# Split operands, values last and ScalarE's division in the cross-attention of a two-layer hybrid block

## The chip, the cores and the metric

The kernel runs on one core of one Trainium2 chip. The metric is device time in microseconds (us) of one execution, the median of several runs. Engines are named as in the profile: PE is TensorE's matmul stream, PEld its weight loads, DVE is VectorE, ACT is ScalarE, POOL is GpSimd, SP is SyncE.

## The reference, cut to what matters

The input is one sequence of 256 tokens with 1024 features, in fp32, and a memory of 256 tokens. Two layers each do a gated feed-forward (FFN), a mixer (layer 0: short convolution with sliding-window attention; layer 1: causal attention), a cross-attention to the memory, and a second FFN. What the change is about is the cross-attention:

```python
def memory_cross_attention(h, mem_n, w_q, w_kv, w_o):     # h: normed x, mem_n: normed memory
    q = (h @ w_q).reshape(B, S, 4, 128)
    kv = (mem_n @ w_kv).reshape(B, M, 2, 4, 128)
    k, v = kv[:, :, 0], kv[:, :, 1]
    logits = jnp.einsum('bshd,bmhd->bhsm', q, k) * 128 ** -0.5
    p = jax.nn.softmax(logits, axis=-1)
    o = jnp.einsum('bhsm,bmhd->bshd', p, v).reshape(B, S, 512)
    return o @ w_o
```

## The kernel before, in words

Activations lie transposed, 128 features by 256 tokens a tile. All projections use **split operands**: an fp32 number is written as hi + lo, both in the type fp32r, and a product is made of three matmuls, hi·hi, hi·lo and lo·hi (`mm_narrow`, L371 to L373; `mm` does the same with a 512-column operand, L366 and L367). ACT makes hi by a copy and DVE makes lo by a subtraction: for weights at L127 and L128, 1024 columns (a block of eight 128x128 weight tiles) at a time with five blocks of buffers, for activations in `split_tile` (L430, L431) and `normed_tile` (L298, L299).

The attentions of `attend` (the memory's in both layers, and that of layer 1's mixer) use plain fp32 operands instead: scores at L613, L614 and L617, transposes of the probabilities (`turn`, L625), values at L633, L635 and L637. An fp32 matmul stands in the trace as two records. The attention of layer 0's mixer, `attend_two`, has split operands already.

A cross-attention stage (`memory`, L918 to L932) has four heads. The order in which it is written out comes from a small planner, `Order`: work with matmuls to do ("fillers") runs in the given order, each with a planned cost in ns, and tasks that must wait for another engine are queued with a delay (`pe.after`). Fillers here: the q projection of heads 0, 1 and 2; the values' projection for all heads (`v_group`, four parts); the q projection of head 3; then the output projection `out_proj`, whose first parts, for four output tiles, use the heads 0 to 2 (`EARLY_XA`). Tasks of each head: scores and softmax; the transposes; the weighing with the values, which is asked for again later as long as the values aren't there; `split_tile` of the result. `norm_scale` is a task too: it makes the norm's factors (`n.rcol`, by token; `n.rbc`, spread over partitions), and q is scaled with `n.rbc` when it leaves PSUM (L924), so a q that comes earlier is parked (L395).

The tile framework then decides the final order on each engine: an instruction may stand ahead of earlier ones that are not ready. Buffers of one name rotate; PSUM has 4 `acc`, 2 `sc` (scores) and 2 `tr` (transposes, weighed results). `p2` has 4 buffers, and `w1` and `w2` are scratch.

Of the kernel before, what the change touches and what calls it, by code (L numbers as in the profile page):

```python
# [23 lines left out]
P = 128  # L24
# [12 lines left out]
XA, EARLY_XA, EARLY_OD = 3, 3, 5  # L37
# [187 lines left out]
def build(nc, tc, ctx, a):  # L225
# [201 lines left out]

    def split_tile(src):
        x2 = Split(act.tile([P, 2 * S], F32R, name="h", bufs=FT))
        nc.scalar.activation(x2.hi, halves(src), AF.Copy)  # L430
        nc.vector.tensor_tensor(x2.lo, halves(src), x2.hi.bitcast(F32), op=ALU.subtract)  # L431
        return x2
# [12 lines left out]
    def ffn(which, layer, n, nxt, first=False, last=False):  # L445
# [29 lines left out]
        def evac(f, g, u):  # L475
# [6 lines left out]
            h[f] = split_tile(u)  # L482
# [84 lines left out]
        if last:  # L567
            xtok = act.tile([P, 2, D], F32, name="bias", bufs=1)
            gfin = act.tile([P, D], F32, name="kT", bufs=2)
# [6 lines left out]
    def softmax(ps, spans, bias, sink):  # L576
# [3 lines left out]
        m = act.tile([P, 2], F32, name="m", bufs=4)  # L580
        neg = act.tile([P, 2], F32, name="neg", bufs=4)
        den = act.tile([P, 2], F32, name="den", bufs=4)
        inv = act.tile([P, 2], F32, name="inv", bufs=4)
        if bias is None:
            nc.vector.tensor_reduce(neg, ps.rearrange("p (t k) -> p t k", t=2), axis=AX.X, op=ALU.max, negate=True)
            src = ps
        else:
            for t, (a0, a1) in enumerate(spans):
                nc.vector.tensor_tensor_reduce(pr[:, a0:a1], ps[t], bias[:, 0 if t else P:], 1.0,
                                               NEG if sink is None else sink, ALU.add, ALU.max, m[:, t:t + 1])  # L590
            nc.vector.tensor_scalar(neg, m, -1.0, None, op0=ALU.mult)
            src = pr
        for t, (a0, a1) in enumerate(spans):
            nc.scalar.activation(pr[:, a0:a1], src[:, a0:a1], AF.Exp, bias=neg[:, t:t + 1], accum_out=den[:, t:t + 1])
        if sink is not None:
            es = act.tile([P, 2], F32, name="es", bufs=4)
# [5 lines left out]
        nc.vector.reciprocal(inv, den)  # L602
        for t, (a0, a1) in enumerate(spans):
# [3 lines left out]
    CAUSAL = ((0, P), (P, 3 * P))  # L607
    FULL = ((0, S), (S, 2 * S))

    def scores(q, k, causal):  # L610
        ps = sc_tile()
        if causal:
            nc.tensor.matmul(ps[:, :P], q[:, :P], k[:, :P], start=True, stop=True)  # L613
            nc.tensor.matmul(ps[:, P:3 * P], q[:, P:], k, start=True, stop=True)  # L614
        else:
            for t in range(2):
                nc.tensor.matmul(ps[:, t * S:(t + 1) * S], q[:, t * P:(t + 1) * P], k, start=True, stop=True)  # L617
        return ps

    def turn(pr, causal):  # L620

        pt = tr_tile()
        blocks = ((0, 0), (1, 1), (2, 2)) if causal else ((0, 0), (1, 2), (2, 1), (3, 3))
        for to, at in blocks:
            nc.tensor.transpose(pt[:, to * P:(to + 1) * P], pr[:, at * P:(at + 1) * P], ident)  # L625
        n = len(blocks) * P
        out = w2()
        nc.scalar.activation(out[:, :n], pt[:, :n], AF.Copy)
        return out

    def weigh(out, v, pT, causal):

        nc.tensor.matmul(out, v(0), pT[:, :S], start=True, stop=False)  # L633
        if causal:
            nc.tensor.matmul(out[:, P:], v(1), pT[:, S:3 * P], start=False, stop=True)  # L635
        else:
            nc.tensor.matmul(out, v(1), pT[:, S:], start=False, stop=True)  # L637

    def attend(heads, done, causal, values=always):


        n = len(heads)
        state = {}

        def go_scores():
            pss = [scores(q, k, causal) for q, k, *_ in heads]
            state["p"] = [softmax([ps[:, a0:a1] for a0, a1 in CAUSAL] if causal else ps, CAUSAL if causal else FULL, b, s)
                          for ps, (_, _, _, b, s, _) in zip(pss, heads)]
            pe.after(2600 + 1500 * n, go_turn, 250 * n)

        def go_turn():
            state["pT"] = [turn(p, causal) for p in state["p"]]
            pe.after(700 + 300 * n, go_weigh, 700 * n)

        def go_weigh():
            if values() == math.inf:
                pe.after(1500, go_weigh, 0)
                return
            out = tr_tile()[:, :S]
            for pT, (_, _, v, _, _, (r0, r1)) in zip(state["pT"], heads):  # L660
                weigh(out[r0:r1], v, pT, causal)
            done(split_tile(out))
            ws.flush()

        pe.after(900, go_scores, 660 * n if causal else 900 * n)
# [3 lines left out]
    def attend_two(q, k2, v2, biases, sinks, done):  # L669
# [6 lines left out]
        def go_scores():  # L676
            q2 = Split(p2())
            nc.scalar.activation(q2.hi, halves(q), AF.Copy)
            nc.vector.tensor_tensor(q2.lo, halves(q), q2.hi.bitcast(F32), op=ALU.subtract)
            both = [sc_tile(), sc_tile()]  # L680
            for t in range(2):
# [7 lines left out]
                                  CAUSAL, biases[s], sinks[s]) for s in range(2)]  # L689
# [73 lines left out]
    def make_bias():  # L763
# [5 lines left out]
        by = act.tile([8, 768], F32, name="kT", bufs=2)  # L769
# [17 lines left out]

    def k_groups(name, layer, c, n, kT, n_heads):
# [5 lines left out]
    made = set()  # L794

    def v_group(name, layer, c, n, v):
        def evac(pss):
            for t, ps in enumerate(pss):
                nc.scalar.activation(v[:, t], ps, AF.Copy, scale=n.rcol[:, t:t + 1])
            made.add(id(v))  # L800
# [3 lines left out]
    def kv_tiles():  # L804
        return (act.tile([P, 4, S], F32, name="kT", bufs=2), act.tile([P, 2, 512], F32, name="v", bufs=2))
# [7 lines left out]
    def kv2_tiles():  # L813

        k = act.tile([P, 4 * S], F32R, name="kT", bufs=2)
# [3 lines left out]
        v = act.tile([P, 2 * S], F32R, name="v", bufs=2)  # L819
        return (k[:, :2 * S], k[:, 2 * S:]), (v[:, :S], v[:, S:])  # L820

    def even_mixer(n, nxt, bias, sinks, kv2, extra):
# [24 lines left out]
        def evac_q(i):  # L847
            def fn(t):
                q = act.tile([P, S], F32, name="q", bufs=2)
# [23 lines left out]
        def evac_b(c):  # L873
            def fn(t):
# [9 lines left out]
                collector(o, c)(split_tile(y))  # L884
# [13 lines left out]
    def odd_mixer(n, nxt, bias, extra):  # L898
# [3 lines left out]
        def evac_q(h):  # L902
            def fn(t):
                q = act.tile([P, S], F32, name="q", bufs=2)
                nc.vector.scalar_tensor_tensor(halves(q), t, 128 ** -0.5, halves(n.rbc), op0=ALU.mult, op1=ALU.mult)
                c = h // 2
                attend([(q, kT[:, c], lambda t: v[:, t, c * P:(c + 1) * P], bias[:, h], None, (0, P))],
                       collector(o, h), True)
# [9 lines left out]
    def memory(layer, n, nxt, kT, v, extra):  # L918
        o = [None] * 4

        def evac_q(h):
            def fn(t):
                q = act.tile([P, S], F32, name="q", bufs=2)
                nc.vector.scalar_tensor_tensor(halves(q), t, 128 ** -0.5, halves(n.rbc), op0=ALU.mult, op1=ALU.mult)  # L924
                attend([(q, kT[:, h], lambda t: v[:, t, h * P:(h + 1) * P], None, None, (0, P))],
                       collector(o, h), False, lambda: 0.0 if id(v) in made else math.inf)
            return fn

        norm_scale(n)
# [47 lines left out]
    kv = {}  # L977

    def mem_keys(layer):

        kv[layer] = kv_tiles()
        pe.after(9000, lambda: [normed_tile(mn, k, m[:, k]) for m in [load_mem()] for k in range(KT)], 0)
        return k_groups("xa_w_kv", layer, 0, mn, kv[layer][0], 4)

    def mem_values(layer):
        return v_group("xa_w_kv", layer, 512, mn, kv[layer][1])

    n, nxt = nxt, xn(("xa_norm", 0))
    even_mixer(n, nxt, bias, sinks, kv2_tiles(), mem_keys(0))
    bias = load_bias(1)  # L990
    n, nxt = nxt, xn(("ffn2_norm", 0))
    memory(0, n, nxt, *kv[0], mem_values(0))
# [7 lines left out]
    memory(1, n, nxt, *kv[1], mem_values(1))  # L1000
# [73 lines left out]
```

## Time and profile before

| | us |
|---|---|
| median of 3 runs | 980.77 (980.58 to 980.92) |
| the profiled execution | 979.29 |
| its span, first to last instruction | 977.2 |
| cross-attention stage, layer 0 (275.06 to 317.05) | 41.99 |
| cross-attention stage, layer 1 (753.15 to 795.14) | 41.99 |

A stage is reckoned here from PE's first matmul on q to its first one of the FFN behind it. Times inside the trace count from the start of the span. The end of a matmul is modelled, so the cost of one matmul in a stream is read from the distance between starts, not from its duration.

### The profile page before, as it was taken

The numbers are of one execution on the slowest core, as the hardware profiler recorded it, in microseconds if no ns is written. First come the engines' busy times: TensorE is split into PE (matmuls) and PEld (weight loads), VectorE is DVE, ScalarE is ACT, GpSimd is POOL, SyncE is SP. The second block draws the span as 40 slices with busy tenths as digits, with TensorE's granted clock in tenths as the row PEclk, the third lists the DMA queues.
The fourth block names the chain that finished last, engine by engine and source line by source line (L and its number), as shares of the span: only waits on it lengthen the run. The fifth ranks groups of instructions, "written<-read, shape, count | busy, mean of one in ns | idle before, by whom it ended". The sixth has DMA issues, their size and how long they took to land.

```text
span 977.2 us, 16591 instructions
## 1 busy us (share of the span) xinstructions
PE 967.6 (99%) x6440; PEld 902.0 (92%) x6440; DVE 755.6 (77%) x1286; ACT 582.6 (60%) x1030; POOL 141.1 (14%) x149
## 2 busy tenths in 40 slices
PE   9999999999999999999999999999999999999997
PEld 8899999999999999999999999999999999999896
DVE  6989777899877978876877887777668678887653
ACT  7766655675556766664556666455665657666542
POOL 3113012202232300002300000221005050000010
PEclk9999999999999999999999999999999999999999
DMA  9897556555553555556556556556545526555531
GB/s 357 297 345 258 186 202 215 174 216 196 191 179 125 194 199 211 202 191 211 199 189 215 186 203 214 185 205 230 181 153 189 176 92 217 210 202 191 210 129 44
DMA packets 28495, 194.70 MB, mean 199 GB/s; under 512 B 3299, under 2 KB 3683, under 8 KB 5761
## 3 DMA queue, kind: packets, MB, share of 16 engines
q1 hardware_dynamic: 27072, 187.71, 55.0%
q0 software_dynamic: 912, 5.37, 1.6%
q8 instruction: 50, 0.82, 0.3%
q10 hardware_dynamic: 432, 0.58, 0.2%
q14 instruction: 29, 0.23, 0.1%
HBM read 192.57 MB, written 4.22 MB: 201 GB/s over the span
## 4 chain that ended last, share of the span: by engine, by line
PE 97%; DMA 1%; ACT 1%; DVE 0%; issue 0%; SPq 0%; POOLq 0%; DVEq 0%
PE acc L366 41%; PE acc L367 20%; PE acc L371 7%; PE acc L373 7%; PE acc L372 7%; PE acc L526 1%; PE acc L525 1%; PE acc L524 1%; DMA raw<-in_w 1%; PE acc L414 1%; PE acc L415 1%; PE acc L416 1%; PE tr L633 1%; PE sc L617 1%; PE tr L625 1%; PE sc L524 0%
## 5 line engine op out<-in xcount | busy, mean ns | idle before, releaser
L128 DVE TENSOR_TENSOR wlo<-raw,whi 128x1024 fp32r<-128x1024 f32 (+2 forms) x357 | 435.6, 1222 | 154.0 <-ACT whi L127 150.9
L127 ACT ACTIVATE whi<-raw 128x1024 fp32r<-128x1024 f32 (+2 forms) x357 | 366.6, 1030 | 296.8 <-PE acc L366 138.4
L366 PE MATMUL acc<-x,whi 128*128 128x512 f32 x1392 | 457.5, 383 | 0.5 <-ACT whi L127 0.4
L367 PE MATMUL acc<-x,wlo 128*128 128x256 f32 x1392 | 377.8, 273 | 0.5 <-DVE wlo L128 0.5
L366 PEld LDWEIGHTS acc<-x,whi 128*128 128x128 f32 x1392 | 262.3, 189 | 37.2 <-ACT whi L127 1.0
L367 PEld LDWEIGHTS acc<-x,wlo 128*128 128x128 f32 x1392 | 267.2, 192 | 1.6 <-DVE wlo L128 0.8
L366 PE MATMUL acc<-h,whi 128*128 128x512 f32 x462 | 151.3, 382 | 0.0
L367 PE MATMUL acc<-h,wlo 128*128 128x256 f32 x462 | 125.4, 273 | 0.0
L366 PEld LDWEIGHTS acc<-h,whi 128*128 128x128 f32 x462 | 87.1, 189 | 11.9
L367 PEld LDWEIGHTS acc<-h,wlo 128*128 128x128 f32 x462 | 88.7, 192 | 0.2
L372 PE MATMUL acc<-h,whi 128*128 128x256 f32 x322 | 88.3, 278 | 0.0
L373 PE MATMUL acc<-h,wlo 128*128 128x256 f32 x322 | 87.5, 276 | 0.0
L371 PE MATMUL acc<-h,whi 128*128 128x256 f32 x322 | 86.3, 279 | 0.9 <-ACT h L430 0.9
L373 PE MATMUL acc<-x,wlo 128*128 128x256 f32 x304 | 84.6, 280 | 0.0
L372 PE MATMUL acc<-x,whi 128*128 128x256 f32 x304 | 83.5, 276 | 0.0
L371 PE MATMUL acc<-x,whi 128*128 128x256 f32 x304 | 82.7, 278 | 0.0
L377 DVE TENSOR_TENSOR w<-acc,w 128x256 f32<-128x256 f32 x195 | 81.2, 417 | 1.1 <-ACT w L376 0.7
L376 ACT ACTIVATE w<-acc 128x256 f32<-128x256 f32 x195 | 71.9, 369 | 4.8 <-PE acc L367 4.7
L306 POOL TENSOR_TENSOR sqacc<-x 128x256 f32<-128x256 f32 x7 | 4.3, 614 | 421.7 <-DVE x L425 421.7
L371 PEld LDWEIGHTS acc<-h,whi 128*128 128x128 f32 x322 | 60.3, 192 | 2.0 <-ACT h L430 1.8
L373 PEld LDWEIGHTS acc<-h,wlo 128*128 128x128 f32 x322 | 61.7, 192 | 0.1
L372 PEld LDWEIGHTS acc<-h,whi 128*128 128x128 f32 x322 | 61.7, 192 | 0.1
(190 smaller groups left out, 1207.2 us busy)
## 6 DMA issues: line engine op xcount, KB each, us to landing
raw<-in_w SPq DMA_DIRECT2D x171, 1024.0 KB, 5.0
dists<-line POOLq DMA_DIRECT2D x2, 1536.0 KB, 12.0
raw<-in_memT SPq DMA_DIRECT2D x3, 1024.0 KB, 5.0
raw<-in_w SPq DMA_DIRECT2D x6, 384.0 KB, 5.8
bias<-dists POOLq DMA_DIRECT2D x2, 1024.0 KB, 10.0
x<-in_xT SPq DMA_DIRECT2D x1, 1024.0 KB, 7.7
kT<-in_final_norm SPq DMA_DIRECT2D x1, 512.0 KB, 3.8
out<-bias ACTq DMA_DIRECT2D x2, 256.0 KB, 2.7
```

The source lines that it names most:

```text
L127: self.nc.scalar.activation(hi[:, at], src, AF.Copy)
L128: self.nc.vector.tensor_tensor(lo[:, at], src, hi[:, at].bitcast(F32), op=ALU.subtract)
L366: nc.tensor.matmul(ps, w[0], x2.both, start=start, stop=False)
L367: nc.tensor.matmul(ps[:, :S], w[1], x2.high, start=False, stop=stop)
L371: nc.tensor.matmul(ps[:, :S], w[0], x2.high, start=start, stop=False)
L372: nc.tensor.matmul(ps[:, :S], w[0], x2.low, start=False, stop=False)
L373: nc.tensor.matmul(ps[:, :S], w[1], x2.high, start=False, stop=stop)
L376: nc.scalar.activation(halves(out), unpaired(ps[:, S:]), AF.Copy)
L377: nc.vector.tensor_tensor(halves(out), unpaired(ps[:, :S]), halves(out), op=ALU.add)
L414: nc.tensor.matmul(ps[t], xh, wh, start=k == 0, stop=False)
L415: nc.tensor.matmul(ps[t], xh, wl, start=False, stop=False)
L416: nc.tensor.matmul(ps[t], xl, wh, start=False, stop=k == KT - 1)
```

## The change

In both cross-attention stages the scores and the weighing use split operands, three fp32r matmuls in place of one fp32 matmul. The memory's keys are split when they are made (in the mixer before), the values when they leave PSUM. q is split straight from PSUM without its scale; the scale goes into the exponential instead. The values' projection comes after all four q. Only two heads may be between their transposes and their weighing (`turned`). In all three attentions ScalarE, not VectorE, multiplies the probabilities by the reciprocals of their sums. Several buffers are made fewer (`sq`, `cg`, `kT`, `v`: 2 to 1), q moves into `w1`, the split values lie in the buffer `bias`, and the bias of layer 1 is therefore loaded after the first cross-attention.

```diff
-        sq = act.tile([P, S], F32, name="sq", bufs=2)
+        sq = act.tile([P, S], F32, name="sq", bufs=1)
...
-    def group(name, layer, c, n, evac):
+    def group(name, layer, c, n, evac, scaled=True):
...
                 if ks[-1] == KT - 1:
                     src = unpaired(ps[:, :S])
+                    if not scaled:
+                        evac(src)
+                        return
...
+    def split_into(x2, src):
+        nc.scalar.activation(x2.hi, src, AF.Copy)
+        nc.vector.tensor_tensor(x2.lo, src, x2.hi.bitcast(F32), op=ALU.subtract)
+        return x2
...
+    def normalize(pr, spans, den):
+        inv = small("inv")
+        nc.vector.reciprocal(inv, den)
+        for t, (a0, a1) in enumerate(spans):
+            nc.scalar.activation(pr[:, a0:a1], pr[:, a0:a1], AF.Copy, scale=inv[:, t:t + 1])
...
-        for t, (a0, a1) in enumerate(spans):
-            nc.vector.tensor_scalar(pr[:, a0:a1], pr[:, a0:a1], inv[:, t:t + 1], None, op0=ALU.mult)
+        normalize(pr, CAUSAL, den)
...
+    def attend_all(n, q2, k2, v2, values, done):
+        def go_scores():
+            ps = state["ps"] = sc_tile()
             for t in range(2):
+                out = ps[:, t * S:(t + 1) * S]
+                qh, ql = (q2.v[:, t, m] for m in range(2))
+                nc.tensor.matmul(out, qh, k2.high, start=True, stop=False)
+                nc.tensor.matmul(out, qh, k2.low, start=False, stop=False)
+                nc.tensor.matmul(out, ql, k2.high, start=False, stop=True)
+            when_scaled(n, soft)
+
+        def soft():
+            ps, pr = state["ps"], w2()
+            neg, den = small("neg"), small("den")
+            nc.vector.tensor_reduce(neg, ps.rearrange("p (t k) -> p t k", t=2), axis=AX.X, op=ALU.max, negate=True)
+            nc.vector.tensor_tensor(neg, neg, n.rs, op=ALU.mult)
+            for t, (a0, a1) in enumerate(FULL):
+                nc.scalar.activation(halves(pr[:, a0:a1]), unpaired(ps[:, a0:a1]), AF.Exp, bias=neg[:, t:t + 1],
+                                     scale=n.rs[:, t:t + 1], accum_out=den[:, t:t + 1])
+            ws.fill()
+            normalize(pr, FULL, den)
+            state["p"] = pr
+            pe.after(4300, go_turn, 450)
 
         def go_turn():
+            if len(turned) > 1:
+                pe.after(500, go_turn, 0)
+                return
+            turned.append(True)
+            pt, pr = tr_tile(), state["p"]
+            for u in range(2):
+                for t in range(2):
+                    nc.tensor.transpose(pt[:, u * S + t * P:u * S + (t + 1) * P], pr[:, t * S + u * P:t * S + (u + 1) * P], ident)
+            state["pT"] = [split_into(Split(p2()), halves(pt[:, u * S:(u + 1) * S])) for u in range(2)]
+            pe.after(1900, go_weigh, 680)
 
         def go_weigh():
             if values() == math.inf:
-                pe.after(1500, go_weigh, 0)
+                pe.after(1300, go_weigh, 0)
                 return
+            turned.pop()
             out = tr_tile()[:, :S]
+            for u, p in enumerate(state["pT"]):
+                vh, vl = v2(u)
+                nc.tensor.matmul(out, vh, p.high, start=u == 0, stop=False)
+                nc.tensor.matmul(out, vh, p.low, start=False, stop=False)
+                nc.tensor.matmul(out, vl, p.high, start=False, stop=u == 1)
+            done(split_tile(unpaired(out)))
             ws.flush()
+        pe.after(1000, go_scores, 680)
...
+    def mem_k_groups(layer, k2):
+                k = w1()
+                nc.vector.tensor_tensor(halves(k), t, halves(mn.rbc), op=ALU.mult)
+                split_into(k2[h], halves(k))
+    def mem_v_group(layer, vh, vl):
+        def evac(pss):
+            for t, ps in enumerate(pss):
+                r = mn.rcol[:, t:t + 1]
+                nc.scalar.activation(vh[:, t], ps, AF.Copy, scale=r)
+                nc.vector.scalar_tensor_tensor(vl[:, t], ps, r, vh[:, t].bitcast(F32), op0=ALU.mult, op1=ALU.subtract)
+            made.add(layer)
...
-                conv[c] = act.tile([P, S], F32, name="cg", bufs=2)
+                conv[c] = act.tile([P, S], F32, name="cg", bufs=1)
...
-    def memory(layer, n, nxt, kT, v, extra):
+    def memory(layer, n, nxt, k2):
         o = [None] * 4
+        v2 = act.tile([P, 2, 2, 512], F32R, name="bias", bufs=1)
...
+            nc.vector.tensor_scalar(n.rs, n.rcol, 128 ** -0.5, None, op0=ALU.mult)
...
-        f = [group("xa_w_q", layer, h * P, n, evac_q(h)) for h in range(4)]
-        f[XA:XA] = [extra]
-        pe.run(list(chain(*f)) + out_proj("xa_w_o", layer, o, nxt, EARLY_XA))
+        f = [g for h in range(4) for g in group("xa_w_q", layer, h * P, n, evac_q(h), scaled=False)]
+        pe.run(f + mem_v_group(layer, v2[:, 0], v2[:, 1]) + out_proj("xa_w_o", layer, o, nxt, EARLY_XA))
...
-    bias = load_bias(1)
-    n, nxt = nxt, xn(("ffn2_norm", 0))
-    memory(0, n, nxt, *kv[0], mem_values(0))
+    memory(0, n, nxt, keys[0])
+    bias = load_bias(1)
```

## Rows read from the trace of the kernel before

**Rows 1.** The page, part 1: busy us, share of the span, instructions.

```profile
PE 967.6 (99%) x6440; PEld 902.0 (92%) x6440; DVE 755.6 (77%) x1286; ACT 582.6 (60%) x1030; POOL 141.1 (14%) x149
```

**Rows 2.** Busy time by stretch: length, then each engine, clock, DMA, GB/s.

```profile
275.06:317.05 41.99, 41.52 (x297) 38.92 (x295) 28.84 (x50) 24.95 (x48) 7.57 (x10) 1.00 0.43 151
753.15:795.14 41.99, 41.52 (x296) 38.92 (x295) 29.04 (x50) 24.83 (x48) 7.74 (x10) 1.00 0.43 151
205.00:235.00 30.00, 30.00 (x256) 29.56 (x256) 29.14 (x95) 21.45 (x58) 4.41 (x6) 1.00 0.51 173
```

**Rows 3.** The timeline of PE, first cross-attention stage, up to the values: start, duration.

```profile
275.06 0.28 PE L371 MATMUL acc<-x,whi 128*128 128x256 f32 x1
...
290.25 1.89 PE L617 MATMUL sc<-kT,q 128*128 128x256 f32 x8
291.79 0.57 PE L414 MATMUL acc<-whi,h 128*128 128x512 f32 x1
292.19 0.38 PE L415 MATMUL acc<-wlo,h 128*128 128x512 f32 x1
...
295.64 0.38 PE L416 MATMUL acc<-whi,h 128*128 128x512 f32 x1
```

**Rows 4.** The timeline of PE, same stage, behind the values, to its end.

```profile
295.86 0.27 PE L371 MATMUL acc<-x,whi 128*128 128x256 f32 x1
...
296.53 1.03 PE L617 MATMUL sc<-kT,q 128*128 128x256 f32 x4
297.39 1.04 PE L625 MATMUL tr<-ident,w 128*128 128x128 f32 x8
...
300.71 0.60 PE L633 MATMUL tr<-w,v 128*128 128x256 f32 x2
...
301.58 1.03 PE L617 MATMUL sc<-kT,q 128*128 128x256 f32 x4
302.44 0.59 PE L633 MATMUL tr<-w,v 128*128 128x256 f32 x2
...
303.12 0.80 PE L371 MATMUL acc<-h,whi 128*128 128x256 f32 x4
303.75 0.60 PE L633 MATMUL tr<-w,v 128*128 128x256 f32 x2
...
304.43 0.46 PE L372 MATMUL acc<-h,whi 128*128 128x256 f32 x1
...
308.62 0.60 PE L633 MATMUL tr<-w,v 128*128 128x256 f32 x2
309.06 0.59 PE L637 MATMUL tr<-w,v 128*128 128x256 f32 x2
310.12 0.71 PE L371 MATMUL acc<-h,whi 128*128 128x256 f32 x4 [0.47 <-ACT h L430]
...
317.05 0.38 PE L366 MATMUL acc<-x,whi 128*128 128x512 f32 x1
```

**Rows 5.** The timeline of ACT, same stage: start, duration, idle before and releaser.

```profile
295.41 1.33 ACT L799 ACTIVATE v<-acc,rcolm 128x512 f32<-128x512 f32 x2 [0.41 <-PE acc L416]
296.65 1.05 ACT L127 ACTIVATE whi<-raw 128x1024 fp32r<-128x1024 f32 x1
...
309.69 0.38 ACT L430 ACTIVATE h<-tr 128x256 fp32r<-128x256 f32 x1 [0.76 <-PE tr L637]
```

**Rows 6.** The timeline of DVE, same stage: the weight split behind the values.

```profile
298.20 1.22 DVE L128 TENSOR_TENSOR wlo<-raw,whi 128x1024 fp32r<-128x1024 f32 x1
```

**Rows 7.** Groups of instructions, whole span: count, busy us, mean ns, idle before.

```profile
L298 ACT ACTIVATE x<-x,vecs 128x256 fp32r<-128x256 f32 x56 | 27.8, 505 | 15.9 <-DVE x L425 15.1
...
L604 DVE TENSOR_SCALAR w<-w,inv 128x256 f32<-128x256 f32 x32 | 10.9, 363 | 0.3
...
L431 DVE TENSOR_TENSOR h<-tr,h 128x256 fp32r<-128x256 f32 x16 | 6.7, 419 | 2.2 <-ACT h L430 2.2
```

**Rows 8.** Line 535 by itself: ns min/median/max of a 512-column DVE instruction from PSUM.

```profile
L535 DVE SCALAR_TENSOR_TENSOR bias<-sc,half_r,bias x1: 750/750/750, 965.3 to 965.3; 128x512 f32<-128x512 f32 x1
```

More of the change, by code (lines that the diff above doesn't have):

```diff
@@ L426, in add_to_x @@
         normed_tile(nxt, j, x[:, j])
+    def split_into(x2, src):
+        nc.scalar.activation(x2.hi, src, AF.Copy)
+        nc.vector.tensor_tensor(x2.lo, src, x2.hi.bitcast(F32), op=ALU.subtract)
+        return x2
     def split_tile(src):
[L429 to L432, printed above, removed]
+        return split_into(Split(act.tile([P, 2 * S], F32R, name="h", bufs=FT)), src)
     def to_tokens(out):
@@ L481, in evac @@
             ws.fill()
-            h[f] = split_tile(u)
+            h[f] = split_tile(halves(u))
             ws.flush()
@@ L568, in ffn @@
             xtok = act.tile([P, 2, D], F32, name="bias", bufs=1)
-            gfin = act.tile([P, D], F32, name="kT", bufs=2)
+            gfin = act.tile([P, D], F32, name="kT", bufs=1)
             src = a["final_norm"]
@@ L601, in softmax, with q2_tile @@
             ws.fill()
-        nc.vector.reciprocal(inv, den)
-        for t, (a0, a1) in enumerate(spans):
-            nc.vector.tensor_scalar(pr[:, a0:a1], pr[:, a0:a1], inv[:, t:t + 1], None, op0=ALU.mult)
-        return pr
[L607 to L612, printed above, removed]
+        normalize(pr, CAUSAL, den)
+        return pr
+    def q2_tile():
+        return Split(act.tile([P, 2 * S], F32R, name="q2", bufs=2))
@@ L613, in scores, with attend @@
+    def attend(q, k, v, bias, done):
+        state = {}
+        def go_scores():
+            ps = sc_tile()
             nc.tensor.matmul(ps[:, :P], q[:, :P], k[:, :P], start=True, stop=True)
             nc.tensor.matmul(ps[:, P:3 * P], q[:, P:], k, start=True, stop=True)
[L615 to L642, printed above, removed]
+            state["p"] = softmax([ps[:, a0:a1] for a0, a1 in CAUSAL], bias, None)
+            pe.after(4100, go_turn, 350)
@@ new lines, in go_turn, with go_weigh @@
+        def go_turn():
+            pt, pT = tr_tile(), w2()
+            for at in range(3):
+                nc.tensor.transpose(pt[:, at * P:(at + 1) * P], state["p"][:, at * P:(at + 1) * P], ident)
+            nc.scalar.activation(pT[:, :3 * P], pt[:, :3 * P], AF.Copy)
+            state["pT"] = pT
+            pe.after(1000, go_weigh, 700)
+        def go_weigh():
+            out = tr_tile()[:, :S]
+            nc.tensor.matmul(out, v(0), state["pT"][:, :S], start=True, stop=False)
+            nc.tensor.matmul(out[:, P:], v(1), state["pT"][:, S:3 * P], start=False, stop=True)
+            done(split_tile(halves(out)))
+            ws.flush()
@@ L768, in make_bias @@
         tab = vecs[:BUCKETS + 1, VCOL["table"]:VCOL["table"] + 8]
-        by = act.tile([8, 768], F32, name="kT", bufs=2)
+        by = act.tile([8, 768], F32, name="kT", bufs=1)
         for h in range(2):
@@ L785, in load_bias, with kv_tiles @@
         return t
+    def kv_tiles():
+        return (act.tile([P, 4, S], F32, name="kT", bufs=1), act.tile([P, 2, 512], F32, name="v", bufs=1))
     def k_groups(name, layer, c, n, kT, n_heads):
@@ L799, in evac, with fn @@
                 nc.scalar.activation(v[:, t], ps, AF.Copy, scale=n.rcol[:, t:t + 1])
-            made.add(id(v))
         return group_tok(name, layer, c, n, evac)
-    def kv_tiles():
-        return (act.tile([P, 4, S], F32, name="kT", bufs=2), act.tile([P, 2, 512], F32, name="v", bufs=2))
+    made = set()
+    def mem_k_groups(layer, k2):
+        def evac(h):
+            def fn(t):
+                k = w1()
+                nc.vector.tensor_tensor(halves(k), t, halves(mn.rbc), op=ALU.mult)
+                split_into(k2[h], halves(k))
+            return fn
+        return [f for h in range(4) for f in group("xa_w_kv", layer, h * P, mn, evac(h))]
+    def mem_v_group(layer, vh, vl):
[5 more added lines that the diff above has]
+            made.add(layer)
+        return group_tok("xa_w_kv", layer, 512, mn, evac)
     def collector(o, i):
@@ L813, in kv2_tiles @@
     def kv2_tiles():
-        k = act.tile([P, 4 * S], F32R, name="kT", bufs=2)
+        k = act.tile([P, 4 * S], F32R, name="kT", bufs=1)
         for s in range(4):
@@ L818, in kv2_tiles @@
             nc.gpsimd.memset(k[r, s * S:(s + 1) * S].bitcast(F32), 0.0)
-        v = act.tile([P, 2 * S], F32R, name="v", bufs=2)
+        v = act.tile([P, 2 * S], F32R, name="v", bufs=1)
         return (k[:, :2 * S], k[:, 2 * S:]), (v[:, :S], v[:, S:])
@@ L848, in fn @@
             def fn(t):
-                q = act.tile([P, S], F32, name="q", bufs=2)
+                q = w1()
                 nc.vector.scalar_tensor_tensor(halves(q), t, 64 ** -0.5, halves(n.rbc), op0=ALU.mult, op1=ALU.mult)
@@ L975, in build @@
     bias, sinks = early["bias"], vecs[:, VCOL["sinks"]:VCOL["sinks"] + 8]
-    kv = {}
     def mem_keys(layer):
-        kv[layer] = kv_tiles()
+        k2 = act.tile([P, 4, 2 * S], F32R, name="k2", bufs=1)
+        keys[layer] = [Split(k2[:, h]) for h in range(4)]
         pe.after(9000, lambda: [normed_tile(mn, k, m[:, k]) for m in [load_mem()] for k in range(KT)], 0)
-        return k_groups("xa_w_kv", layer, 0, mn, kv[layer][0], 4)
-    def mem_values(layer):
-        return v_group("xa_w_kv", layer, 512, mn, kv[layer][1])
+        return mem_k_groups(layer, keys[layer])
+    keys = {}
     n, nxt = nxt, xn(("xa_norm", 0))
     even_mixer(n, nxt, bias, sinks, kv2_tiles(), mem_keys(0))
+    n, nxt = nxt, xn(("ffn2_norm", 0))
+    memory(0, n, nxt, keys[0])
     bias = load_bias(1)
-    n, nxt = nxt, xn(("ffn2_norm", 0))
-    memory(0, n, nxt, *kv[0], mem_values(0))
     n, nxt = nxt, xn(("ffn1_norm", 1))
@@ L999, in build @@
     n, nxt = nxt, xn(("ffn2_norm", 1))
-    memory(1, n, nxt, *kv[1], mem_values(1))
+    memory(1, n, nxt, keys[1])
     ffn("ffn2", 1, nxt, None, last=True)
```

67 lines of the change are left out of this document (27 added, 40 removed).

## Prediction

> **What bounds the kernel now.** I read the page first: PE is busy 967.6 of 977.2 us [rows 1], so time can come only out of PE's own work or its few waits, and work moved between VectorE and ScalarE counts only where PE comes to wait for it. Next the stretches [rows 2]. The two cross-attention stages take 41.99 us each, with the same 0.47 us of PE idle in each (41.99 less 41.52), so I cost one and double it. The stretch of layer 0's attention, 205 to 235, shows the opposite picture: PE never idles though VectorE is busy 29.14 of 30 us and ScalarE 21.45. Last I read PE's timeline of the first stage, by distances between starts [rows 3, 4], and what ScalarE and VectorE do where the values end [rows 5 to 8].
>
> **What PE saves.** Between 295.86 and 296.53 stand six split matmuls of 256 columns [rows 4]: 0.67/6 = 0.11 us each. The fp32 scores stand at 290.25 to 291.79 (two heads), 296.53 to 297.39 and 301.58 to 302.44: 1.54 + 0.86 + 0.86 = 3.26 us [rows 3, 4]. The fp32 weighing stands at 300.71 to 301.58, 302.44 to 303.12, 303.75 to 304.43 and 308.62 to 310.12: 0.87 + 0.68 + 0.68 + 1.50 = 3.73 us, the last with the stage's wait of 0.47 in it [rows 4]. Sum 6.99 us. After the change each head has six matmuls for scores and six for weighing: 4 x 12 x 0.11 = 5.3 us. Saved: 1.7 us, the old wait included.
>
> Three times the stream pays for going from fp32 back to split operands. The distance 291.79 to 292.19 is 0.40 us where a matmul of 512 columns has 0.22 (295.64 to 295.86) [rows 3, 4]; four matmuls take 303.12 to 303.75 = 0.63 in place of 0.45; the one at 304.43 is shown with 0.46 in place of 0.28 [rows 4]. These are 0.18 each, 0.55 us. They go with the fp32 matmuls; the transposes stay fp32, and what they cost now they cost then. The saving is 1.7 + 0.55 = 2.2 us a stage, 4.5 us in both.
>
> **What PE loses: the values come last.** Today the fourth q's projection stands behind the values' last matmul, from 295.86 on, and the values leave PSUM (295.41 to 296.74) under it [rows 4, 5]. After the change no projection stands there. By the planner's costs, heads 0 and 1 are transposed while the values are projected, and two heads is the limit; behind the values come the weighing of heads 1 and 0, the transposes of 2 and 3, their weighing, then the output projection. All of it hangs on the split values. Count from the values' last matmul, 295.86 in today's times:
>
> - ScalarE makes hi for the first token half by +0.22 and for the second by +0.88 (two copies, 1.33 from 295.41) [rows 5]. VectorE's lo, from PSUM with 512 columns, is not in this stage; the nearest row has 0.75 [rows 8]. So lo is there at +0.97 and +1.72.
> - The two weighings are 12 matmuls, 1.33 us. Ten of them fit in before +1.72; the last two end their issue at +1.94.
> - A result reaches ScalarE 0.04 after the matmul's shown end (309.06 + 0.59 = 309.65, the copy starts at 309.69) [rows 4, 5]. The last matmul starts at +1.83, lasts 0.28 as others of this size, so at +2.15 the copies begin, 0.38 each: hi of one head at +2.53, of the other at +2.91. The output projection begins with head 0, the second of the two.
> - From 0 to +2.91 PE has 1.33 us to do: idle 1.58 us. The transposes of head 2 can't fill it, since both `tr` buffers are given to the two weighings.
> - From +2.91 there are 4 matmuls of the output projection with hi of head 0 (0.45 us, to +3.35). More needs a lo, which is 0.42 of VectorE each [rows 7], at +2.95 and +3.37 if VectorE is free. Today a weight split of 1.22 starts 2.34 after the values' end [rows 6]; if one lies there again, the first lo is at +3.98, and PE idles 0.6 more.
>
> So 1.6 to 2.2 us of new idle time a stage. I take 2.0, since the weight block that the values free is due just there. Behind it no wait should follow: the output projection's first two inputs are 24 matmuls, 2.7 us, which cover the splits of the probabilities of heads 2 and 3 (0.38 and 0.42 a half) before their weighing. That the order is mixed in this way is seen at 303.12, where four matmuls of the output projection stand before the third head's weighing [rows 4]. And the old wait at 310.12 is gone, as head 3 is done before the second parts.
>
> Sum of a stage: 41.99 - 2.2 + 2.0 = 41.8, so -0.2, and -0.4 in both.
>
> **The other parts.** Each softmax gives two scalings (0.36 each for 256 columns) from VectorE to ScalarE, where the nearest row, a scaled copy out of SBUF, has 0.505 [rows 7]: 48 instructions in the kernel. Splitting keys, q and probabilities adds one ScalarE and one VectorE instruction of about 0.4 a tile. In the stages themselves VectorE has 13 us free and ScalarE 17 [rows 2], so they cost nothing there but the chain above. In layer 0's attention 16 of the scalings come onto ScalarE: at most 16 x 0.505 = 8 us on 21.45 of 30 [rows 2]; VectorE gets room. As PE did not wait with VectorE at 97%, I take nothing; without that cover it would be a rival, below. q unscaled lets the scores start earlier, but PE does not wait for them now: nothing. The fewer buffers: `sq` is used on POOL in order, `cg` is rewritten a whole group later, `kT` and `v` are done with one stage before the next user; nothing, and where one did bind, the norm's factors would be some tenths late, which the FFN's first groups cover. The bias load goes past the first cross-attention on POOL's queue, behind the weighing and beside the squares of the norm, and has two FFNs until its use. A dearer weighing from a moving operand with interleaved halves is excluded: today's 0.11 us matmuls read the same layout.
>
> **The rivals.**
>
> *The hole fills itself* (0.20). If the transposes of heads 2 and 3 get buffers before the weighings, their 0.86 us (eight transposes take that from 297.39 on) run inside the hole. New idle 1.1 us, the stage -1.1, both -2.2: 978.6 by the median. For it: the order is made by readiness. Against it: buffers of one name rotate, and `p2` holds two heads only.
>
> *The hole goes on* (0.13): slower. If the output projection's matmuls are not put ahead of the second pair's weighing, PE waits for that chain too: from the `tr` buffer free at +3.4, transposes 0.45, the copies and subtractions of both halves 1.25, weighing 0.67, hi 0.4: +6.2, against 1.33 + 0.86 + 0.67 + some 0.3 of the fourth weighing. Idle 3.0 to 3.6 us, the stage +0.8 to +1.4; with the weight split in the way 0.6 more. Both: +2.2 to +4, some 983.5. It decides from 3.2 us of idle a stage on. The trace speaks against it with the mixing at 303.12 [rows 4]. The Trainium skill (TensorE: Matmul & The Clock Gate, section "Step-by-step: what each phase is for") says that PE pulls weight loads ahead but runs its matmuls in program order; by that, a weighing that waits holds up all ready matmuls of the output projection behind it, and this rival's time is what results where the written order has them behind. The trace agrees so far as it goes: at 310.12 PE sat idle until one hi came.
>
> *ScalarE becomes the bound in layer 0's attention* (0.07): slower. With 8 us more it has 29.5 of 30; its weight splits then come late and PE waits for a block. One or two splits late are 1 to 2 us: with the main case 982. It decides once ScalarE's share there is full. The Trainium skill (VectorE: DVE Perf Modes, section "The perf-mode tier table (the rule you actually need)") says that fp32 scaling from SBUF runs at twice the rate of a two-operand instruction on VectorE, so the move would be a poor trade; the rows don't bear the factor out, 363 ns against 419 for the two-operand one [rows 7]. By the page's rule ScalarE gains more work than VectorE loses, by the rows the same.
>
> **How the numbers follow.** The profiled execution is 979.29, its span 977.2, so 2.1 lie around the span; the sum gives 978.9 for such an execution. The median shown is 980.77, 1.5 above; so 980.4. About 0.2% (2 us) is what a measurement can tell from no change: under 978.8 is faster, over 982.7 slower. Main case, idle 1.2 to 3.0 a stage: -2 to +1.6, that is 978.8 to 982.4, chance 0.60. Faster 0.20, same 0.60, slower 0.20 (0.13 + 0.07). The range reaches half-way into both sides: 978.0 to 983.0.
>
> **What would show it.** Right: the stages at 41 to 42.5 us; fp32 scores and weighing gone, 96 records of 0.11 us in their place; the first idle spell of a stage 1.5 to 2.2 us, behind the values' last matmul, ended by the values' lo and by hi of a result; no idle at the second parts of the output projection. Wrong: idle before the second pair's weighing, PE waiting for whi in layer 0's mixer, or the transposes of heads 2 and 3 inside the values' projection.

## The result, and the profile after

| | before | after |
|---|---|---|
| median of 13 runs each, us | 980.21 (979.61 to 980.92) | 985.96 (982.41 to 987.59) |
| ratio, 95% interval | | 1.0052 (1.0040 to 1.0063) |
| span of the profiled execution | 977.2 | 980.7 |
| cross-attention stages | 41.99, 41.99 | 43.84, 43.84 |
| layer 0's mixer, first matmul on its input to the stage | 92.19 | 91.97 |

The forecast was no change, 980.4, with a range of 978.0 to 983.0. The kernel is slower by half a percent, outside the range. The 13 executions are of two kinds: four took 982.41 to 983.51, with a mean granted TensorE clock of 0.998 to 0.999; nine took 985.66 to 987.59, with one of 0.993 to 0.995. All executions of the kernel before whose clock was listed have 0.998 or 0.999. The profiled execution is of the first kind (982.52). So there are two losses: about 3 us which the profiled execution shows, and 3 to 5 us more that come and go with the clock. At the full clock alone the kernel would have ended at 982.4 to 983.5, at the upper edge of the range.

The page, part 1, and the busy time by stretch (length, then PE, PEld, DVE, ACT, POOL, clock, DMA) of the changed kernel, against [rows 1, 2]:

```profile
PE 966.2 (99%) x6472; PEld 901.2 (92%) x6472; DVE 754.5 (77%) x1276; ACT 603.1 (61%) x1098; POOL 138.4 (14%) x149
```

```profile
275.13:318.97 43.84, 40.77 (x312) 38.38 (x311) 31.36 (x57) 29.32 (x62) 8.38 (x11) 1.00 0.48 169
754.92:798.76 43.84, 40.77 (x313) 38.38 (x311) 31.34 (x57) 29.25 (x62) 7.41 (x10) 1.00 0.41 145
205.00:235.00 30.00, 30.00 (x257) 29.60 (x256) 27.59 (x83) 26.67 (x73) 3.32 (x5) 1.00 0.44 147
```

PE's busy time in a stage fell (41.52 to 40.77), as split operands should do; its idle time went from 0.47 to 3.07 us. Layer 0's attention shows the opposite: ScalarE rose from 21.45 to 26.67 of 30 us and PE still never waits. So the profiled loss is all in the two stages, 1.85 us each (3.7 us, where the span grew by 3.5). PE's timeline there, first stage of the changed kernel (start, duration, idle before and releaser), answers to [rows 4]:

```profile
299.58 0.38 PE L420 MATMUL acc<-whi,h 128*128 128x512 f32 x1
...
300.22 0.38 PE L420 MATMUL acc<-whi,h 128*128 128x512 f32 x1
302.11 0.38 PE L697 MATMUL tr<-p,bias 128*128 128x256 f32 x1 [1.51 <-ACT bias L857]
302.33 0.28 PE L698 MATMUL tr<-p,bias 128*128 128x256 f32 x1
...
302.55 0.28 PE L698 MATMUL tr<-p,bias 128*128 128x256 f32 x1
302.90 0.38 PE L699 MATMUL tr<-p,bias 128*128 128x256 f32 x1
...
304.69 0.71 PE L371 MATMUL acc<-h,whi 128*128 128x256 f32 x4 [0.64 <-ACT h L434]
305.24 1.08 PE L685 MATMUL tr<-ident,w 128*128 128x128 f32 x8
...
312.39 0.28 PE L373 MATMUL acc<-h,wlo 128*128 128x256 f32 x1
313.51 0.38 PE L371 MATMUL acc<-h,whi 128*128 128x256 f32 x1 [0.85 <-DVE x L429]
```

The L420 at 299.58 is the last matmul of the values' first token half, the one at 300.22 that of the second half. L697 to L699 are the weighing, L685 the transposes. PE waits 1.51 us for hi of the values, a little behind 302.55 for their lo, 0.64 for hi of the first result, and 0.85 behind 312.39 for an `acc` buffer that the addition to x (L429) must free. As distances between starts, each less the time that the matmul has in an unbroken stream (0.22 for 512 columns, 0.11 for 256), these spells are 1.67, 0.24, 0.80 and 1.01: 3.7 us in place of the 2.0 forecast. The second stage has the same four. ScalarE's timeline shows why the first is so long, against [rows 5]:

```profile
299.36 1.06 ACT L127 ACTIVATE whi<-raw 128x1024 fp32r<-128x1024 f32 x1
300.31 0.39 ACT L434 ACTIVATE p<-tr 128x256 fp32r<-128x256 f32 x1
300.57 0.91 ACT L591 ACTIVATE w<-w,inv 128x256 f32<-128x256 f32 x2
301.37 1.27 ACT L857 ACTIVATE bias<-acc,rcolm 128x512 fp32r<-128x512 f32 x2
```

The first half of the values was there at 299.96 (299.58 + 0.38), but its copy (L857) starts at 301.37, with no idle time before it: ScalarE works off a weight split, a split of probabilities and two divisions (L591, 0.91) first. Before the change ScalarE sat idle for 0.41 us waiting for the values; now the values wait for it. VectorE's timeline, with a weight split behind the values and then the last spell:

```profile
303.62 1.23 DVE L128 TENSOR_TENSOR wlo<-raw,whi 128x1024 fp32r<-128x1024 f32 x1
...
311.89 1.23 DVE L128 TENSOR_TENSOR wlo<-raw,whi 128x1024 fp32r<-128x1024 f32 x1 [1.12 <-ACT whi L127]
313.04 1.41 DVE L429 TENSOR_TENSOR x<-acc,x 128x256 f32<-128x256 f32 x4
```

At the last spell four output tiles, to which only the last head was missing, end close together, and a weight split of 1.23 us stands before the additions that free their buffers.

### The profile page after: what moved, and what is told of

It is laid out like the page before. It is cut to its first block, busy times and chain, and to the rows that moved or that the text cites. A ratio compares the mean times of both kernels' runs of the same rounds, so it can differ in the third digit from the quotient of the medians.

```text
span 980.7 us, 16723 instructions
## 1 busy us (share of the span) xinstructions
PE 966.2 (99%) x6472; PEld 901.2 (92%) x6472; DVE 754.5 (77%) x1276; ACT 603.1 (61%) x1098; POOL 138.4 (14%) x149
## 4 chain that ended last, share of the span: by engine, by line
PE 94%; ACT 2%; DVE 1%; DMA 1%; issue 0%; SPq 0%; POOLq 0%; DVEq 0%
PE acc L366 41%; PE acc L367 20%; PE acc L371 7%; PE acc L373 7%; PE acc L372 7%; PE acc L533 1%; PE acc L532 1%; PE acc L531 1%; DMA raw<-in_w 1%; ACT whi L127 1%; PE acc L420 1%; PE acc L418 1%; PE acc L419 1%; DVE wlo L128 1%; PE sc L531 0%; PE sc L532 0%
```

## The experiments

**Theory A:** the values' place opens holes in PE's stream, ScalarE's divisions lengthen them (A2, formed after the first four runs: what counts is what stands in ScalarE's queue), and holes bring the clock down. **Rivals** are named in the expectations. Ratios in brackets are 95% intervals against the kernel before, which took 979.6 to 979.7 us beside these runs.

**1. The changed kernel once more** (no edit). 

> The changed kernel itself once more, to see whether its executions fall into two levels and what sets them apart. Theory A (holes and clock): PE waits 3.7 us in each cross-attention stage, and in most executions the granted clock is lower for a while behind those holes; executions near 982.5 have a mean clock of 0.998 or more, those near 986 one of 0.995 or less, and a profile of the second kind shows the low clock behind 300 and 780 us of the span and nowhere else. Rival B (the split operands or the fuller ScalarE lower the clock or the pace at large): a profile of the second kind shows it spread over the span or in the mixers.

Median 982.98; ratio 1.0043 (1.0030 to 1.0056). Three executions took 982.55 to 982.98 at a clock of 0.998 or 0.999, two 985.61 and 985.94 at 0.996 and 0.995. The profiled execution is of the second kind. Its busy time by stretch: the second stage, and the part of it at the low clock.

```profile
755.02:801.72 46.70, 43.63 (x313) 41.26 (x311) 31.34 (x57) 29.21 (x62) 7.41 (x10) 0.93 0.39 136
783.90:790.60 6.70, 6.06 (x29) 6.01 (x29) 3.11 (x7) 2.07 (x6) 0.00 (x0) 0.50 0.27 111
```

Its timeline of PE there (start, duration):

```profile
783.57 0.39 PE L699 MATMUL tr<-p,bias 128*128 128x256 f32 x2
784.59 1.22 PE L371 MATMUL acc<-h,whi 128*128 128x256 f32 x4 [0.64 <-ACT h L434]
...
787.53 0.42 PE L373 MATMUL acc<-h,wlo 128*128 128x256 f32 x1
787.74 0.42 PE L371 MATMUL acc<-h,whi 128*128 128x256 f32 x1
```

The granted clock is 0.50, the lower level of 1.2 GHz, for nearly 7 us, from about 783.8 on: behind the first two spells, with the third (783.8 to 784.6) just begun. Matmuls stand 0.21 apart there in place of 0.11. This stage takes 46.70 us in place of 43.84; the first stage of the same execution, with the same spells, stayed at the full clock and took 43.85. This fall costs 2.85 us. Theory A holds for where it falls; 982.5 is no fall and 985.6 one, so 987 is likely two, which no trace shows.

**2. The values third, as before.** 

> The changed kernel with one part undone: the values' projection stands before the fourth q again, all else as changed. Theory A: the fourth q's projection (2.7 us) covers the values on their way out of PSUM, the first spell of 1.5 us is gone, at most 1 us of idle stays near the fourth head, a stage takes 40.5 to 41.8 us, the clock stays at 0.998 to 0.999 in nearly all executions, time 977 to 980.5. Rival B: the clock still falls, time 983 or more.

```diff
-        pe.run(f + mem_v_group(layer, v2[:, 0], v2[:, 1]) + out_proj("xa_w_o", layer, o, nxt, EARLY_XA))
+        f[6:6] = mem_v_group(layer, v2[:, 0], v2[:, 1])
+        pe.run(f + out_proj("xa_w_o", layer, o, nxt, EARLY_XA))
```

Median 985.55 (ratio 1.0049 to 1.0074): no better, and three of five at a clock of 0.996. The place of the values alone is not it: here Theory A failed, and A2 replaced it. A stage takes 44.73 us. PE's timeline shows a new first wait, the split of the fourth q:

```profile
302.50 0.38 PE L659 MATMUL sc<-k,q 128*128 128x256 f32 x1 [1.53 <-ACT q L434]
```

and ScalarE's shows what stood before that split:

```profile
300.29 0.94 ACT L591 ACTIVATE w<-w,inv 128x256 f32<-128x256 f32 x2
301.09 1.08 ACT L127 ACTIVATE whi<-raw 128x1024 fp32r<-128x1024 f32 x1
302.04 0.41 ACT L434 ACTIVATE q<-acc 128x256 fp32r<-128x256 f32 x1
```

**3. VectorE divides, everywhere.** 

> The changed kernel with one part undone: VectorE divides by the sums, as before the change, in all three attentions; the values still come last. Theory A: the copies of the values leave ScalarE 1 to 1.6 us earlier, the first spell shrinks from 1.5 to about 0.3 to 0.7 us, a stage takes 42 us or a little less; time 979.5 to 981 where the clock holds, and it falls in fewer executions than with the change. If ScalarE's divisions do nothing (rival C: only the place of the values counts): first spell still 1.5 us, time as the changed kernel, 982.4 to 987.

```diff
-            nc.scalar.activation(pr[:, a0:a1], pr[:, a0:a1], AF.Copy, scale=inv[:, t:t + 1])
+            nc.vector.tensor_scalar(pr[:, a0:a1], pr[:, a0:a1], inv[:, t:t + 1], None, op0=ALU.mult)
```

Median 981.06 (1.0006 to 1.0023), eleven executions of 980.46 to 981.95, all at 0.998 or 0.999. A stage takes 42.63 us, 1.21 less than with ScalarE; the first spell is 0.29 by distance. Rival C falls.

**4. The kernel before with the values last alone.** 

> The kernel before with one part of the change alone: the values' projection behind all four q; fp32 operands and VectorE's division stay. Theory A: a hole opens behind the values (they must leave PSUM, 1.3 us, and a result must be split), 1 to 2.5 us a stage, time 981 to 984 where the clock holds, and the clock may fall in some executions. Rival B: as the operands are the old ones, no lower clock in any execution, and a time of 980 to 981.

```diff
-XA, EARLY_XA, EARLY_OD = 3, 3, 5
+XA, EARLY_XA, EARLY_OD = 4, 3, 5
```

Median 989.20 (1.0084 to 1.0119), worse than expected. The stages take 47.23 and 45.89 us. The stretch of 306.7 to 309.6, in the fp32 weighing, is at the lower clock:

```profile
275.79:323.02 47.23, 44.18 (x296) 40.08 (x295) 28.87 (x50) 24.66 (x48) 7.55 (x10) 0.96 0.39 134
759.23:805.12 45.89, 42.77 (x297) 38.74 (x295) 29.04 (x50) 24.55 (x48) 7.72 (x10) 1.00 0.41 138
306.70:309.60 2.90, 2.90 (x8) 2.36 (x7) 0.53 (x2) 0.77 (x2) 0.00 (x0) 0.50 0.00 0
```

So the clock falls behind holes with the old operands too, and rival B falls. But its long waits, in PE's timeline, are not for the values:

```profile
304.10 0.72 PE L625 MATMUL tr<-ident,w 128*128 128x128 f32 x4 [1.31 <-DVE w L604]
305.92 0.70 PE L633 MATMUL tr<-w,v 128*128 128x256 f32 x2 [1.10 <-ACT w L628]
```

PE waits for VectorE's division of a late head, and then for ScalarE's copy of its transposed probabilities. So the hole is not the one that Theory A had in mind, and this run does not price the place of the values by itself. The profiled execution has a mean clock of 0.998 in spite of its fall of some 3 us: a mean of 0.998 alone does not exclude a short fall.

**5. Values third and VectorE divides.** 

> The changed kernel with two parts undone: the values' projection before the fourth q, and VectorE divides. The run with the values third alone left PE waiting 1.5 us a stage for ScalarE's split of the fourth q, behind exponentials, divisions and copies in ScalarE's queue. Theory A2 (ScalarE's queue sets the holes, the place of the values decides what is queued): with 0.9 us a head taken off ScalarE that wait goes to under 0.7 us, all holes of a stage add up to 2 to 3 us, time 979 to 981.5, the clock holds. Rival D (values third is bad by itself with split operands, the chain of the fourth head is too long): holes stay at 4 us or more, time 983 or more.

The edits of runs 2 and 3 together. Median 983.40 (1.0025 to 1.0050), clock 0.998 or 0.999; a stage takes 43.71 us. Taking the divisions off ScalarE gains 1.0 us a stage here as well, but PE still waits 1.0 us for the fourth q's split and again at the end of that head's chain. The idle time, 2.2 us a stage, is as Theory A2 said, the time is rival D's: with split operands and VectorE's division the values do better behind the last q (run 3, 42.63 us a stage).

**6. Matmuls in the hole.** 

> The changed kernel plus 12 matmuls of 256 columns in each stage behind the values' last matmul, whose result nobody reads; they take 1.3 us of the first spell of 1.5 us, so that PE is not idle there while everything else waits as before. Theory A (the idle spells bring the clock down): no or fewer executions with the low clock, time 982 to 983.5 in at least four of five. Rival E (the clock falls with something else, for example the start of denser matmuls): both levels as with the changed kernel, 982.5 and 985.5 to 987, and the twelve matmuls change nothing.

```diff
+        def keep_busy():
+            ps = sc_tile()
+            for i in range(12):
+                nc.tensor.matmul(ps[:, :S], n.x[0].v[:, 0, 0], n.x[0].high, start=i == 0, stop=i == 11)
-        pe.run(f + mem_v_group(layer, v2[:, 0], v2[:, 1]) + out_proj("xa_w_o", layer, o, nxt, EARLY_XA))
+        pe.run(f + mem_v_group(layer, v2[:, 0], v2[:, 1]) + [(always, keep_busy, 0)]
+               + out_proj("xa_w_o", layer, o, nxt, EARLY_XA))
```

Median 982.49, seven executions of 982.22 to 982.81, all at 0.998. The stage is as long as with the change, 43.84, but PE is not idle in the first spell; its timeline:

```profile
300.23 1.50 PE L995 MATMUL sc<-x 128*128 128x256 f32 x12
301.90 0.38 PE L697 MATMUL tr<-p,bias 128*128 128x256 f32 x1 [0.17 <-ACT bias L857]
```

Of 18 executions of the changed kernel (13 and run 1's five) 11 had the lower clock; of these seven none. Work added to PE makes the kernel 3.5 us faster than the changed one at the median of its 13 executions. Rival E falls as far as seven executions can tell: the changed kernel itself was not timed beside them, so that they met other conditions than its 18 is not excluded by this run alone. Run 3, timed beside run 1 and with less idle PE, had no fall in eleven either. Together they point to idle PE as what brings the clock down.

**7. The kernel before with ScalarE's divisions alone.** 

> The kernel before with one part of the change alone: ScalarE divides by the sums in all three attentions. Theory A2: ScalarE is full only where copies of the values, splits and exponentials meet; with fp32 operands there are fewer copies, so 0 to 1 us a stage more, 979.7 to 982, the clock mostly holds. Rival C2 (ScalarE's division costs nothing by itself, the rows showed it 60% busy): 979.5 to 980.

```diff
-            nc.vector.tensor_scalar(pr[:, a0:a1], pr[:, a0:a1], inv[:, t:t + 1], None, op0=ALU.mult)
+            nc.scalar.activation(pr[:, a0:a1], pr[:, a0:a1], AF.Copy, scale=inv[:, t:t + 1])
```

Median 982.84 (1.0023 to 1.0048), clock 0.998 or 0.999. By stretch, the first stage and layer 0's mixer:

```profile
275.93:319.21 43.28, 42.14 (x297) 39.05 (x296) 26.68 (x42) 27.75 (x56) 7.75 (x10) 1.00 0.43 147
183.17:275.93 92.76, 92.30 (x803) 91.25 (x802) 79.95 (x177) 64.41 (x134) 18.98 (x20) 1.00 0.55 193
```

The stage is 1.29 longer and the mixer 0.57: a full 3 us from this part alone, more than Theory A2 said. Rival C2 falls, though ScalarE is busy only 27.75 of 43.28 us in the stage. PE's longest wait there is 0.52 us for VectorE's q of the last head (L924) and not for the values, so this run shows that the divisions cost, and runs 3 and 9 show through what.

**8. Values second, VectorE divides.** 

> The changed kernel with VectorE dividing and the values' projection behind two of the four q: two projections of q (5.3 us) then stand behind the values. Theory A2: the values are split and the first two heads are weighed under the third and fourth q; the fourth head's chain is the only one exposed, holes of a stage under 2 us, time 976.5 to 979, under the kernel before. Rival D (the chain of the last head is too long with split operands, wherever the values stand): holes of 3 us or more, 981 or more.

Run 3 with the values' projection put in by `f[4:4] = mem_v_group(...)`. Median 983.12 (1.0022 to 1.0047), a stage 43.58: rival D's time. PE's idle time is only 1.53 us there, as Theory A2 said, but in more and smaller waits, which by distances between starts add up to some 3 us.

**9. VectorE divides in the cross-attentions only.** 

> The changed kernel with one part undone in one place: VectorE divides in the two cross-attentions alone; in the mixers ScalarE divides as changed. Theory A2 (what hurts is ScalarE's queue in front of the values' copies): a stage takes 42.6 us as with VectorE dividing everywhere, the mixer of layer 0 92.0 us as with the change, time 980 to 981, the clock holds. Rival F (the divisions in the mixers cost as well): 982 or more.

Run 3's edit for `attend_all` alone. Median 980.24; ratio 1.0005 (0.9996 to 1.0014): no change that can be measured. The stages and layer 0's mixer, by stretch:

```profile
275.28:317.91 42.63, 40.72 (x313) 38.51 (x311) 33.58 (x65) 26.45 (x54) 8.36 (x11) 1.00 0.50 173
753.85:796.49 42.64, 40.72 (x312) 38.52 (x311) 33.59 (x65) 26.35 (x54) 7.42 (x10) 1.00 0.43 148
183.31:275.28 91.97, 91.97 (x803) 91.19 (x801) 82.25 (x181) 65.36 (x138) 17.48 (x19) 1.00 0.53 184
```

ScalarE's timeline behind the values, where it is idle again until they come:

```profile
298.82 1.09 ACT L127 ACTIVATE whi<-raw 128x1024 fp32r<-128x1024 f32 x1
300.13 1.33 ACT L860 ACTIVATE bias<-acc,rcolm 128x512 fp32r<-128x512 f32 x2 [0.23 <-PE acc L420]
301.37 1.05 ACT L127 ACTIVATE whi<-raw 128x1024 fp32r<-128x1024 f32 x1
```

The divisions in the changed kernel's mixers cost nothing on ScalarE (91.97, against 92.60 on VectorE in run 3). In the kernel before they cost 0.57 there (run 7); why the sign differs was not followed. With those in the two stages back on VectorE the kernel's time can't be told from that of the kernel before, though the trace still has 0.64 us more in each stage. Rival F falls.

**10 to 12. Attempts to close the other spells**, all on run 9's kernel. Run 10 is the first of them:

> The run before this one (VectorE divides in the cross-attentions) with the first parts of the output projection over two heads in place of three. The last spell of a stage, 0.85 us on VectorE's addition to x, comes from four output tiles that end 0.33 us apart, since only the fourth head was missing to them, on a VectorE that needs 0.42 for one and has a weight split before them. With two heads missing they end 0.67 apart. Theory G: the spell of 1 us goes, a stage takes 41.6 to 41.9 us, time 978 to 979.5. Rival H (the spell is the weight split alone, whatever the distance): as the run before, 980 to 981.

```diff
-EARLY_XA, EARLY_OD = 3, 5
+EARLY_XA, EARLY_OD = 2, 5
```

Median 980.16 (0.9997 to 1.0014), a stage 42.66. The wait for the addition to x is gone from the list of waits, but one of 0.61 for lo of a result stands in its place at 310.04. The time is rival H's, the reason neither theory's: the spell moved.

Run 11 has this edit on the kernel of run 12 below, with the values in pieces too:

> The same with the transposes of the probabilities in the PSUM buffers of the scores, and no limit of two heads: the transposes of heads 2 and 3 need not wait for a weighed result to leave its buffer, so their 0.9 us can run inside the values' projection. Theory: the spell of 0.8 us before the first result is not shorter by itself, but 0.9 us of work leaves the stretch behind it, which was covered already; gain 0 to 0.5 us a stage, time 977.5 to 979.5. Rival: with more heads under way ScalarE's queue fills again before the values' copies, and a stage takes 42.5 us or more.

```diff
-            if len(turned) > 1:
-                pe.after(500, go_turn, 0)
-                return
             turned.append(True)
-            pt, pr = tr_tile(), state["p"]
+            pt, pr = sc_tile(), state["p"]
```

Median 982.49 (1.0018 to 1.0038), a stage 43.62, which is 0.50 more than in run 12: the rival's time. PE waits for splits of the probabilities there (0.68 for ScalarE's hi, 0.57 and 0.49 for VectorE's lo), not for the values. One of its eight executions has a clock of 0.997, the others 0.998 or 0.999.

Run 12:

> The run with two heads first, and the values leave PSUM in four pieces of 256 columns in place of two of 512, heads 0 and 1 first. Theory A: the first two weighings wait for half the values, lo of both token halves is there 0.5 to 0.6 us earlier, the first two spells (0.3 and 0.5 us) go; a stage takes 41.0 to 41.4 us, time 977 to 978.5. Rival: the shorter instructions' own fixed cost, and the copies of the second half in the way of the results' copies, eat it: 978 to 979.5 as without.

```diff
-            for t, ps in enumerate(pss):
...
-                nc.scalar.activation(vh[:, t], ps, AF.Copy, scale=r)
...
+            for c in range(2):
+                at = slice(c * 256, (c + 1) * 256)
+                for t, ps in enumerate(pss):
...
+                    nc.scalar.activation(vh[:, t, at], ps[:, at], AF.Copy, scale=r)
```

VectorE's line is changed likewise, and run 10's edit is in. Median 981.40 (1.0008 to 1.0026), a stage 43.12. PE's wait for the first hi of the values (0.13 us in run 10) is gone and the one for their lo a little shorter (0.24 for 0.30), but the wait for the results' copies is longer (0.75 for 0.64) and the next output matmuls start up to 0.39 us apart: it is slower than both theory and rival said, in the rival's direction. No version that was tried beats the kernel before.

## Why the prediction was wrong, point by point

- **What bounds the kernel, what PE saves:** right in the sum. The stretches showed PE full; fp32 scores and weighing and the returns to split operands were worth 2.2 us a stage by the forecast. One reading in it is wrong, without harm: the returns cost nothing of their own. At each the last fp32 record starts only 0.03 us before the split matmul behind it, where the other records of 256 columns stand 0.22 apart, so the 0.18 is the rest of that record's time, which the forecast's distances had left out. In run 9 the stage is 42.63 us, with 2.6 us of spells by distance (0.29, 0.46, 0.80, 1.01): without them 40.1, where 41.99 less 2.2 gives 39.8.
- **The hole behind the values:** the mechanism was right in its place. Without ScalarE's divisions (run 9) it was so in its size too: the first three spells are 1.55 us, where 1.6 to 2.2 were forecast, ended by hi and lo of the values and by hi of a result. In the changed kernel the longest, 1.67, is ended by the values' hi, which the forecast had ready at once. The weight split that was to cost 0.6 more did stand before the results' lo (303.62 to 304.85), but no wait is seen for it, since eight transposes ran on PE from 305.24 on, which the forecast's count left out. "Behind it no wait should follow" was wrong: 1.01 us of waiting for the addition to x came later.
- **ScalarE's divisions: the step that failed.** The forecast took them at nothing, since ScalarE has 17 us free in a stage and they "cost nothing there but the chain above", and then left them out of that chain: it let the values' copies start at once, 0.45 us before the end of the values' stream. They started 0.93 behind it (301.37, against 300.22 + 0.22), since the divisions of a late head stood before them in ScalarE's order. Measured: 1.2 us a stage (runs 3 and 9 against the change), and 1.3 with the divisions alone (run 7). The free time was elsewhere in the stage.
- **The clock: the rival that was missing.** All cases were priced at the full clock, as [rows 2] showed 1.00 in every stretch. With 3.7 us of spells in a stage it falls in 11 of 18 executions, at 2.85 us for the fall that a trace shows. The median, 985.96, is made of that and the stages; without the falls the time would have been near the upper edge of the range. The forecast's slower rivals (the second pair's weighing, ScalarE in layer 0's mixer) both did not occur; layer 0's mixer took 91.97 against 92.19.
- **VectorE's rate:** the factor of two that the forecast cites from the Trainium skill (VectorE: DVE Perf Modes, section "The perf-mode tier table (the rule you actually need)") stayed unused. That table is for 2048 elements; the 363 and 419 ns compared with it are of instructions of 256, the second reading PSUM, so they neither bear it out nor speak against it. What decided was which engine's queue stands before the values, not the price of one division.

The sum with what was measured: 41.99 - 2.2 + 3.7 = 43.5 a stage against 43.84. Part of the 0.3 left is seen behind the spells, where the first two matmuls start 0.21 to 0.22 apart in place of 0.11 (302.11 and 302.33). From the forecast's 41.8 the way is + 1.2 for the divisions, + 1.0 for the wait for the addition to x, + 0.3, and - 0.45 because the hole without the divisions was 1.55 and not 2.0.

## What to carry to other kernels

An engine's free time over a stage says nothing about a queue that is worked off in order: before moving work onto an engine, list what stands in its queue ahead of the instruction that PE waits for next. A PE-bound kernel can pay for an idle spell twice, as this one did: once as waiting and, in some executions, once more at half the clock behind it. So executions at two levels with different mean clocks are a reason to look for holes. And filling a hole with useless matmuls is a cheap test of whether the second price is being paid.

## What the runs showed of the hardware that was not expected

No single spell before a fall of the clock was long. In run 1 PE had idled 1.51 and then some 0.2 us between 780.1 and 783.8, with matmuls at full clock before, between and behind the two spells; then the granted clock was 0.50, the 1.2 GHz level, until about 790.7. Behind the same spells in the first stage of that execution it stayed at 1.00. The Trainium skill (TensorE: Matmul & The Clock Gate, section "A second HAM failure mode: psum-queue depth-cycling") tells of another kernel in which small idle times between groups of matmuls make the clock swing between its two levels; the traces agree, with 2.85 us lost by one such swing. Why one stage falls and the other does not, with the same instructions, no run here settles.
